# Attention on one core: the values' rounded and rest halves as one stationary tile, two products instead of three

## The chip, the cores and the metric

One core of a Trainium2 chip runs the whole program as one launch. The metric is the device time of that launch in microseconds (us), lower is better. Three runs of the kernel before took 1016.07, 1016.13 and 1017.07 us; their median is 1016.13.

The engines are called by the profile's names: PE is TensorE (its weight loads are listed apart as PEld), DVE is VectorE, ACT is ScalarE, POOL is GpSimd. Each runs its instructions in the order in which they were written into its queue and waits at semaphores for the others.

## The reference

A decoder trunk of two layers on 512 tokens of width 1024: a gated short convolution with a SwiGLU block, then an attention layer with a second SwiGLU block. Only the attention matters here. It has 16 heads of 64 columns; four heads share one of 4 key and value heads; a token sees the 128 tokens up to itself, and a sink joins the softmax.

```python
kk, vv = with_prev(k), with_prev(v)          # per block of 128: the block before and this one
scores = jnp.einsum('bnqhgd,bnkhd->bnhgqk', qb, kk).astype(jnp.float32) * scale
scores = jnp.where(valid[None, :, None, None], scores, NEG)
probs = jax.nn.softmax(jnp.concatenate([scores, sink], axis=-1), axis=-1)[..., :-1]
out = jnp.einsum('bnhgqk,bnkhd->bnqhgd', probs.astype(v.dtype), vv)
```

Everything is float32.

## The kernel before, in words

Each float32 operand of a product is cut into a rounded half, which ScalarE writes in the type fp32r, and a rest half, which VectorE makes by subtracting. A product of two operands is then three products (`mm3`, lines 193 to 195): rounded by rest, rounded by rounded, rest by rounded. Rest by rest is dropped.

The attention runs by pairs of heads. The heads are ordered so that pair t (of eight) holds two heads e = 0, 1 that use two neighbouring value heads. A loop of ten steps, i = 0 to 9, is written as one string, `ORDER`; each word of it is one piece of work of one pair, and the word order is the order in every engine's queue. In step i the words do the following:

- `R-` rotates the query projection of pair i + 1: on VectorE a shuffle (L1261) and a multiply (L1263), both reading the projection's PSUM tile, then two operations on POOL (L1267, L1270). `H-` splits the rotated queries (L1280 on ScalarE, L1281 on POOL).
- `S0`, `S1` are the scores of pair i, two halves of two PSUM tiles `psc`, one for each head (L1334). `M` masks and takes the maxima on VectorE (L1346), `E` the exponents on ScalarE (L1362, L1369), `N` divides by the sums on VectorE (L1374 to L1379).
- `T0` to `T3` transpose the probabilities of pair i - 1, one key block each (L1391), into the PSUM tiles `pt`; `P` writes their rounded half on ScalarE (L1404), `L` the rest half on VectorE (L1408).
- `W0` to `W3` (`weigh`) are the value products of pair i - 1, one key block each: per block and head three products of 128 x 256 into one PSUM tile `po`. The stationary tile is 128 wide though a head has 64 value columns: the value tiles `vt` hold zeros between the heads, so that head 0 fills the upper 64 partitions of `po` and head 1 the lower 64, each adding zeros to the other's. Thus 24 products a pair.
- `O-` (`out`) reads the finished `po` of pair i - 2 and writes its rounded half (ACT, L1428) and rest half (DVE, L1429), the operands of the output projection.
- `Q` projects the queries of pair i + 2 into a tile `pq`; `Z` and `z` (steps 5 to 8) compute the part of the output projection that needs only the first four pairs, and copy it out (L1446, `mixo`); `G`, `g`, `A` split weights ahead (L182 to L189, L420, L425).

For the steps in `NEXT` (0, 1, 2, 3, 4, 6, 7) `S1` is moved up behind `S0`, and its two tiles then come from the pool `ps_mm`; otherwise from `ps_sc`. `ps_mm` has four banks. It serves `S1` in those steps, `Q`, `Z` and `po`. A tile gets the bank that has been given back longest, and its first product waits until the last reader of the tile before it is done. `pt` has two banks of its own, `S0` two.

After the loop `close` finishes the output projection with pairs 4 to 7 (PSUM tiles `pmix`), pair 7 last.

## Time and profile before

| | us |
|---|---|
| median of three runs | 1016.13 (1016.07 to 1017.07) |
| profiled execution, span from its first to its last instruction | 1014.9 |
| between that span and the median: start and end around the instructions, since no separate device time is given for the profiled execution | 1.2 |
| PE busy in the span | 1007.0 (99%) |
| DVE, ACT, POOL busy | 867.8, 580.4, 193.8 |
| the loop's steps 1 to 8, first score product of step 1 to last value product | 555.31 to 653.67 |
| mean granted TensorE clock | 0.998 |

Times inside the execution count from the first instruction. In a row of the order of time the first number is the start, the second the duration, then engine, line, operation, output and inputs; `x4` merges four that follow each other, and square brackets give idle time ahead of it and what ended it. Matmuls overlap, so their pace is the distance between starts and not the duration. In a table by windows, each engine has its busy time and its number of instructions, and then come the granted clock, the share of DMA time and GB/s.

### The profile page before, as it was taken

To read this page: it belongs to the slowest core of one execution; us is meant where nothing else is said; L and a number is where in the kernel's file an instruction comes from. 1 tells how busy PE (TensorE), PEld (TensorE's weight loads), DVE (VectorE), ACT (ScalarE), POOL (GpSimd) and SP (SyncE) were. 2 spreads that over 40 slices of the span, in tenths; PEclk is the share of its full clock that TensorE was granted. 3 is DMA by queue.
4 is the path that set the end of the run, shared out by engine and by line. 5 is a ranking of instruction groups with operands and counts; after the bars stand their busy time and mean duration, and the time that the engine had idled before them with its cause. 6 is when DMAs were issued, how large, how long until landed. Compare 5 with 4: busy or idle time off the path is not lost.

```text
span 1014.9 us, 16253 instructions
## 1 busy us (share of the span) xinstructions
PE 1007.0 (99%) x6008; PEld 893.2 (88%) x6008; DVE 867.8 (86%) x1480; ACT 580.4 (57%) x1035; POOL 193.8 (19%) x259
## 2 busy tenths in 40 slices
PE   9999999999999999999999999999999999999997
PEld 8888888999889898998898888889998998989986
DVE  5766768899788999998878998779997899999896
ACT  6322544875656455566484786677666564645641
POOL 0443133102101011000032753221111010110001
PEclk9999999999999999999999999999999999999999
DMA  9897789549979789779603889976989676979842
GB/s 353 289 246 242 184 253 337 176 166 269 340 238 291 241 285 321 239 212 336 203 2 136 215 241 271 252 276 151 279 282 333 170 248 225 300 263 263 266 155 84
DMA packets 66576, 244.50 MB, mean 241 GB/s; under 512 B 7873, under 2 KB 8385, under 8 KB 54721
## 3 DMA queue, kind: packets, MB, share of 16 engines
q1 hardware_dynamic: 51328, 145.98, 38.8%
q0 software_dynamic: 14592, 96.48, 37.6%
q10 hardware_dynamic: 576, 1.02, 0.3%
q8 instruction: 47, 0.77, 0.3%
q14 instruction: 33, 0.26, 0.1%
HBM read 237.15 MB, written 102.76 MB: 335 GB/s over the span
## 4 chain that ended last, share of the span: by engine, by line
PE 99%; DVE 1%; issue 0%; DVEq 0%
PE gx L1072 15%; PE gx L1075 8%; PE gz L195 4%; PE gz L193 4%; PE gz L194 4%; PE pcub L193 4%; PE pcub L195 4%; PE pcub L194 4%; PE px L193 4%; PE px L194 4%; PE px L195 4%; PE pmix L193 3%; PE pmix L195 3%; PE pmix L194 3%; PE gy L195 2%; PE gy L194 2%
## 5 line engine op out<-in xcount | busy, mean ns | idle before, releaser
L479 DVE TENSOR_TENSOR wlo<-raw,whi 128x1024 fp32r<-128x1024 f32 x225 | 274.6, 1225 | 53.6 <-ACT whi L478 53.4
L478 ACT ACTIVATE whi<-raw 128x1024 fp32r<-128x1024 f32 x225 | 233.6, 1051 | 100.7 <-DVE raw L466 28.9
L1072 PE MATMUL gx<-xt,whi 128*128 128x512 f32 x480 | 120.4, 393 | 0.0
L1072 PEld LDWEIGHTS gx<-xt,whi 128*128 128x128 f32 x480 | 86.3, 189 | 15.5
L547 POOL DMA_DIRECT2D hsum<-in_w_gb_dram x96 | 62.8, 733 | 150.6 <-ACT whi L478 90.1
L547 POOL DMA_DIRECT2D hsum<-hsum x32 | 25.3, 790 | 295.5 <-ACT whi L478 198.2
L1034 DVE TENSOR_TENSOR st<-gx,st 128x256 f32<-128x256 f32 x200 | 78.0, 419 | 2.5 <-ACT st L1050 0.4
L1050 ACT ACTIVATE st<-gx 128x256 f32<-128x256 f32 x120 | 43.4, 380 | 62.6 <-PE gx L1075 58.9
L1075 PEld LDWEIGHTS gx<-xt,wlo 128*128 128x128 f32 x480 | 65.5, 190 | 4.7
L1075 PE MATMUL gx<-xt,wlo 128*128 128x256 f32 x480 | 66.9, 282 | 0.0
L1086 ACT ACTIVATE gr<-gr 128x1024 f32<-128x1024 f32 x20 | 21.2, 1062 | 49.9 <-DVE gr L1034 49.9
L193 PE MATMUL px<-wlo,ahi 128*128 128x512 f32 x120 | 46.7, 389 | 0.0
L194 PE MATMUL px<-whi,ahi 128*128 128x512 f32 x120 | 46.7, 389 | 0.0
L195 PE MATMUL px<-whi,alo 128*128 128x512 f32 x120 | 46.7, 389 | 0.0
L195 PE MATMUL gz<-xhi,wlo 128*128 128x256 f32 x160 | 45.5, 284 | 0.0
L193 PE MATMUL gy<-xlo,whi 128*128 128x256 f32 x160 | 45.3, 283 | 0.0
L194 PE MATMUL gy<-xhi,whi 128*128 128x256 f32 x160 | 45.3, 283 | 0.0
L195 PE MATMUL gy<-xhi,wlo 128*128 128x256 f32 x160 | 45.3, 283 | 0.0
L193 PE MATMUL gz<-xt,whi 128*128 128x256 f32 x160 | 45.3, 283 | 0.0
L194 PE MATMUL gz<-xt,whi 128*128 128x256 f32 x160 | 45.3, 283 | 0.0
L195 PE MATMUL gz<-xt,wlo 128*128 128x256 f32 x160 | 45.3, 283 | 0.0
L193 PE MATMUL gz<-xlo,whi 128*128 128x256 f32 x160 | 45.3, 283 | 0.0
(298 smaller groups left out, 2989.0 us busy)
## 6 DMA issues: line engine op xcount, KB each, us to landing
hsum<-in_w_gb_dram POOLq DMA_DIRECT2D x96, 512.0 KB, 7.8
raw<-hsum SPq DMA_DIRECT2D x88, 512.0 KB, 8.0
raw<-in_w_gb_dram SPq DMA_DIRECT2D x60, 512.0 KB, 7.0
hsum<-in_w_dn_dram POOLq DMA_DIRECT2D x36, 512.0 KB, 8.0
raw<-in_w_dn_dram SPq DMA_DIRECT2D x32, 512.0 KB, 6.3
hsum<-hsum POOLq DMA_DIRECT2D x28, 512.0 KB, 5.6
raw<-in_w_in_dram SPq DMA_DIRECT2D x21, 512.0 KB, 7.4
hsum<-in_w_dn_dram POOLq DMA_DIRECT2D x12, 768.0 KB, 12.9
```

What stands on the lines that cost most here:

```text
L193: nc.tensor.matmul(out, whi, xlo, start=start, stop=False, **kw)
L194: nc.tensor.matmul(out, whi, xhi, start=False, stop=False, **kw)
L195: nc.tensor.matmul(out, wlo, xhi, start=False, stop=stop, **kw)
L478: self.begun = nc.scalar.activation(hi[:, :n], raw, AF.Copy)
L479: nc.vector.tensor_tensor(out=lo[:, :n], in0=raw, in1=hi[:, :n].bitcast(F32), op=ALU.subtract)
L547: nc.gpsimd.dma_start(dst, src, max_dma_last_dim=4 * 4 * S, **kw))
L1034: nc.vector.tensor_tensor(out=out, in0=a, in1=b, op=ALU.add)
L1050: nc.scalar.activation(ste, a, AF.Copy)
L1072: nc.tensor.matmul(banks[c][e], whi[:, kk], factors[p][k][2], start=opened and k == 0, stop=False, **kw)
L1075: nc.tensor.matmul(banks[c][e][:, :256], wlo[:, kk], factors[p][k][0], start=False, stop=k == 3 and p == 4, **kw)
L1086: nc.scalar.activation(kept[2], kept[2], AF.Silu)
```

## The change

The value tiles change their layout. For each pair of value heads (g) a tile now holds four groups of 64 columns: rounded half of head 0, rest of head 0, rest of head 1, rounded of head 1. There are no zeros left, so the eight memsets of `vt` on POOL go, and four tiles of 128 x 512 hold what eight held. ScalarE writes groups 0 and 3 and VectorE groups 1 and 2 of each, in as many instructions as before.

One stationary tile of a head is now its rounded and its rest columns side by side. `weigh` multiplies it with the rounded probabilities and then with the rest ones: two products a head and block, 16 a pair, and rest by rest is now included. Each head has its own PSUM tile: for head 0 the upper 64 partitions hold the rounded values' part and the lower 64 the rest values' part, for head 1 the other way round.

A new piece, `join`, stands where `out` stood (`O-`): ScalarE copies the part of each tile that lies on the other half of the partitions across into an SBUF tile `o` (64 x 512, twice), and VectorE adds the part that lies where it belongs (64 x 512, twice). `out` (now `o-`) follows three words later, behind `M0` and `Q1`, and reads `o` in SBUF where it read `po` in PSUM.

```diff
-    "R- S0 T0 T1 O- Q0 M0 Q1 Z0 P0 P1 S1 ...
+    "R- S0 T0 T1 O- Q0 M0 Q1 o- Z0 P0 P1 S1 ...
...
         def weigh(self, j):
             if j == 0:
-                self.po = bank("po", ps_mm)
+                self.po = [bank("po", ps_mm) for _ in range(2)]
             hk = 2 * (self.t // 4)
-            phi, plo = self.turned[j][:2]
             q = min(j, NB - 2) * P
+            for i, p in enumerate(self.turned[j][:2]):
+                for e in range(2):
+                    nc.tensor.matmul(self.po[e][:, q : q + 256],
+                                     vt[j][:, (hk + e) * P : (hk + e + 1) * P],
+                                     p[:, e * 256 : (e + 1) * 256], start=i == j == 0,
+                                     stop=i == 1 and j == NB - 1, skip_group_check=True)
+
+        def join(self):
+            self.o = wide("o")[:, :S]
+            rows = [slice(e * HD, (e + 1) * HD) for e in range(2)]
             for e in range(2):
-                vc = slice((2 * hk + e) * HD, (2 * hk + 2 + e) * HD)
-                pc = slice(e * 256, (e + 1) * 256)
-                mm3(self.po[:, q : q + 256], vt[j][0][:, vc], vt[j][1][:, vc],
-                    phi[:, pc], plo[:, pc], j == 0 and e == 0, j == NB - 1 and e == 1,
-                    skip_group_check=True)
+                nc.scalar.activation(self.o[rows[e]], self.po[e][rows[1 - e]], AF.Copy)
+            for e in range(2):
+                nc.vector.tensor_tensor(out=self.o[rows[e]], in0=self.po[e][rows[e]],
+                                        in1=self.o[rows[e]], op=ALU.add)
...
-            nc.scalar.activation(hi, self.po, AF.Copy)
-            nc.vector.tensor_tensor(out=lo, in0=self.po, in1=hi.bitcast(F32), op=ALU.subtract)
+            nc.scalar.activation(hi, self.o, AF.Copy)
+            nc.vector.tensor_tensor(out=lo, in0=self.o, in1=hi.bitcast(F32), op=ALU.subtract)
...
-        vt = [halves("vt", F32R) for _ in range(NB)]
-        for pair in vt:
-            for v in pair:
-                nc.gpsimd.memset(v.bitcast(F32), 0.0)
+        vt = [v for _ in range(NB // 2) for v in halves("vt", F32R)]
...
-            nc.scalar.activation(dst[j][0], src[j], AF.Copy)
+            nc.scalar.activation(dst[j][:, :, 0::3], src[j], AF.Copy)
...
-            nc.vector.tensor_tensor(out=dst[j][1], in0=src[j], in1=dst[j][0].bitcast(F32),
-                                    op=ALU.subtract)
+            nc.vector.tensor_tensor(out=dst[j][:, :, 1:3], in0=src[j],
+                                    in1=dst[j][:, :, 0::3].bitcast(F32), op=ALU.subtract)
```

Two places show how the instructions move. A name's number tells tiles apart; `[waits ...]` names the engines on whose progress the instruction waits.

On TensorE, at the scores of step 2: where the second half's two tiles (from `ps_mm`) are opened and their next two products, before:

```order
L1334 MATMUL psc_5953<-rlo_5583,rhl_5869 128x256
L1334 MATMUL psc_5954<-rlo_5583,rhl_5869 128x256
L1334 MATMUL psc_5953<-rhi_5582,rhl_5869 128x256
L1334 MATMUL psc_5954<-rhi_5582,rhl_5869 128x256
L1334 MATMUL psc_5953<-rhi_5582,rhl_5869 128x256
```

and now:

```order
L1334 MATMUL psc_5936<-rlo_5573,rhl_5859 128x256
L1334 MATMUL psc_5937<-rlo_5573,rhl_5859 128x256 [waits DVE_49]
L1334 MATMUL psc_5936<-rhi_5572,rhl_5859 128x256
L1334 MATMUL psc_5937<-rhi_5572,rhl_5859 128x256
L1334 MATMUL psc_5936<-rhi_5572,rhl_5859 128x256
```

The second tile has gained a wait on VectorE. With `po` in two banks, the bank that it gets is that of the projection of step 1, which VectorE reads in this step's `R-`; in steps 3 and 4 it is the same.

On VectorE, the start of step 2, before (the second half of each row of maxima is a short instruction that reads an accumulator):

```order
L1261 STREAM_SHUFFLE sh_5932<-pq_5808 128x512 [waits PE_49]
L1263 TENSOR_TENSOR ra_5934<-pq_5808,ctab_5215 128x512 [waits PE_49]
L1429 TENSOR_TENSOR ohl_5981<-po_5891,ohl_5981 128x512 [waits Activation_49]
L1346 ISA s_5992,nm_5991<-psc_5939,mask,nsnk 128x128 [waits PE_49]
L1346 ISA nm_5991 128x1
```

and now, down to the rest half of the first transposed block:

```order
L1261 STREAM_SHUFFLE sh_5915<-pq_5798 128x512 [waits PE_49]
L1263 TENSOR_TENSOR ra_5917<-pq_5798,ctab_5215 128x512 [waits PE_49]
L1428 TENSOR_TENSOR o_5964<-po_5881,o_5964 64x512 [waits Activation_49]
L1428 TENSOR_TENSOR o_5964<-po_5882,o_5964 64x512 [waits Activation_49]
L1346 ISA s_5977,nm_5976<-psc_5922,mask,nsnk 128x128 [waits PE_49]
L1346 ISA nm_5976 128x1
L1346 ISA s_5978,nm_5976<-psc_5923,mask,nsnk 128x128 [waits PE_49]
L1346 ISA nm_5976 128x1
L1346 ISA s_5977,nm_5976<-psc_5922,mask,nsnk 128x256
L1346 ISA nm_5976 128x1
L1346 ISA s_5978,nm_5976<-psc_5923,mask,nsnk 128x256
L1346 ISA nm_5976 128x1
```

The two adds of the join stand where the rest half of the output stood, and that comes next after these rows, behind the maxima, as L1437. On ScalarE the two copies (L1426) stand where the rounded half (L1428) stood, and the rounded half follows them at once (L1436), ahead of the probabilities' rounded halves.

More of the change, by code (lines that the diff above doesn't have):

```diff
@@ L47 @@
 ORDER = (
-    "R- S0 T0 T1 O- Q0 M0 Q1 Z0 P0 P1 S1 T2 T3 L0 Q2 L1 G M1 E00 E01 k H- g0 Q3 P2 P3 E10 E11 Z1 z0 W0 L2 L3 A A A N0 W1 W2 N1 W3 g1 z1"
+    "R- S0 T0 T1 O- Q0 M0 Q1 o- Z0 P0 P1 S1 T2 T3 L0 Q2 L1 G M1 E00 E01 k H- g0 Q3 P2 P3 E10 E11 Z1 z0 W0 L2 L3 A A A N0 W1 W2 N1 W3 g1 z1"
 )
@@ L52 @@
     "S": "scores", "M": "maxima", "E": "exponents", "N": "normalise", "T": "turn", "P": "high",
-    "L": "low", "W": "weigh", "O": "out", "Q": "project", "R": "rotate", "H": "split",
+    "L": "low", "W": "weigh", "O": "join", "o": "out", "Q": "project", "R": "rotate", "H": "split",
     "G": "weights", "Z": "project", "z": "out",
@@ L1521, in yoco_kernel @@
         qs[0].rotate(nc.vector)
-        dst = [[v.rearrange("p (h d) -> p h d", d=2 * HD)[:, :, :HD] for v in pair]
-               for pair in vt]
-        src = [p.rearrange("p (h d) -> p h d", d=HD) for p in pv]
+        dst = [v.rearrange("p (g a d) -> p g a d", g=2, d=HD) for v in vt]
+        src = [p.rearrange("p (g e d) -> p g e d", g=2, d=HD) for p in pv]
         for j in range(NB):
-            nc.scalar.activation(dst[j][0], src[j], AF.Copy)
+            nc.scalar.activation(dst[j][:, :, 0::3], src[j], AF.Copy)
         for j in range(NB):
@@ L1563, in yoco_kernel @@
                     continue
-                if op in "SMENTPLWO":
-                    t -= op in "TPLWO"
+                if op in "SMENTPLWOo":
+                    t -= op in "TPLWOo"
                     of = hp
```

## The prediction

> **What bounds the kernel now.** I read the page's head and its chain that ended last, then the loop over the head pairs as a table by step, then the order of time inside one step.
>
> ```profile
> span 1014.9 us, 16253 instructions
> PE 1007.0 (99%) x6008; PEld 893.2 (88%) x6008; DVE 867.8 (86%) x1480; ACT 580.4 (57%) x1035; POOL 193.8 (19%) x259
> PE 99%; DVE 1%; issue 0%; DVEq 0%
> ```
>
> TensorE sets the end nearly everywhere, so fewer products should be time won. But these shares are means. The windows below run from a step's first score product to the next one's: rows 1 to 7 are steps 1 to 7 of the loop, the last row is step 8.
>
> ```profile
> core 0: us, PE busy (x) PEld busy (x) DVE busy (x) ACT busy (x) POOL busy (x), PEclk, DMA share, GB/s
> 555.31:567.00 11.69, 11.69 (x87) 10.34 (x86) 11.48 (x42) 8.05 (x28) 7.85 (x8) 1.00 0.85 244
> 567.00:578.69 11.69, 11.69 (x87) 10.36 (x86) 11.55 (x38) 8.38 (x27) 7.54 (x7) 1.00 0.88 247
> 578.69:590.39 11.70, 11.70 (x87) 10.36 (x86) 11.32 (x38) 8.88 (x28) 6.96 (x7) 1.00 0.92 197
> 590.39:602.17 11.78, 11.78 (x87) 10.41 (x86) 11.52 (x36) 10.01 (x29) 7.48 (x9) 1.00 0.64 164
> 602.17:619.61 17.44, 17.44 (x113) 14.85 (x112) 14.61 (x48) 9.91 (x31) 8.44 (x7) 1.00 1.03 345
> 619.61:631.49 11.88, 11.88 (x89) 10.41 (x88) 10.33 (x32) 10.17 (x32) 3.10 (x4) 1.00 0.88 209
> 631.49:643.38 11.89, 11.89 (x87) 10.36 (x87) 10.76 (x38) 10.21 (x32) 3.44 (x5) 1.00 1.01 290
> 643.38:653.67 10.29, 10.20 (x65) 8.83 (x63) 8.05 (x17) 7.52 (x12) 2.12 (x4) 1.00 0.96 276
> ```
>
> In steps 1 to 4 TensorE is busy throughout, and VectorE for all but 0.2 to 0.4 us of 11.7: two engines are full at once. Only steps 5 to 8 leave VectorE 1.1 to 2.8 us. So what the change adds to VectorE counts as much as what it takes from TensorE.
>
> **What it removes.** The value products, in order of time and by count:
>
> ```profile
> 565.84 0.28 PE L193 MATMUL po<-plo,vt 128*128 128x256 f32 x1
> 565.96 0.28 PE L194 MATMUL po<-phi,vt 128*128 128x256 f32 x1
> L193 PE MATMUL po<-plo,vt x48: 277/283/387, 564.0 to 652.6; 128*128 128x256 f32 x48
> L193 PE MATMUL po<-lp,vt x16: 280/283/283, 566.2 to 653.3; 128*128 128x256 f32 x16
> ```
>
> One lasts 0.28 us but the next starts 0.12 later, and that pace is the price. Lines 193 to 195 hold 64 each; the change leaves 128 of 192, so it takes 64 x 0.12 = 7.7 us, 0.96 a pair, in steps 1 to 8. The new products have the same shape and one weight load each; I keep the pace.
>
> Eight memsets on POOL go too. They are worth nothing: behind them POOL waits 24.7 us for VectorE's first rotation.
>
> ```profile
> 519.50 3.79 POOL L1503 MEMSET vt<- 128x512 f32 x8
> 548.97 1.29 POOL L1267 TENSOR_TENSOR sh<-sh,stab 128x512 f32<-128x512 f32 x1 [24.74 <-DVE sh L1261]
> ```
>
> The split of the values keeps its eight instructions and sizes: nothing.
>
> **What it adds to VectorE.** Step 2 shows the places, and the starts of the rotation in steps 3 to 5:
>
> ```profile
> 567.64 0.74 DVE L1261 STREAM_SHUFFLE sh<-pq 128x512 f32<-128x512 f32 x1
> 567.82 0.28 PE L1334 MATMUL psc<-rlo,rhl 64*128 64x256 f32 x2
> 568.27 0.68 DVE L1263 TENSOR_TENSOR ra<-pq,ctab 128x512 f32<-128x512 f32 x1
> 568.86 0.69 DVE L1429 TENSOR_TENSOR ohl<-po,ohl 128x512 fp32r<-128x512 f32 x1
> 569.46 0.35 DVE L1346 CUSTOM_DVE_ANT_0 s<-psc,mask,nsnk 128x128 f32<-128x128 f32 x1
> 570.81 1.29 DVE L1408 TENSOR_TENSOR plo<-pt,phi 128x512 fp32r<-128x512 f32 x2
> 579.31 0.75 DVE L1261 STREAM_SHUFFLE sh<-pq 128x512 f32<-128x512 f32 x1
> 591.02 0.74 DVE L1261 STREAM_SHUFFLE sh<-pq 128x512 f32<-128x512 f32 x1
> 604.67 0.75 DVE L1261 STREAM_SHUFFLE sh<-pq 128x512 f32<-128x512 f32 x1
> ```
>
> The low half of the output (L1429) takes 0.60 us, from 568.86 to the next start. It stays, only later. The two adds of the join have its 512 columns and one PSUM operand, on 64 partitions. No row shows 64 partitions on VectorE: below, 0.30 each if time went by elements; above, the whole 0.69. I take 0.60, since a row's columns pass one after another whatever the partitions. So 1.2 us a pair, first in step 2 (the join comes two steps behind its scores). VectorE's idle time there, 0.1 in step 2 and 0.3 to 0.4 in the next two, can't hold it, and I leave that idle time where it is, because it ends on other engines' work. So its chain grows by 1.2 in each of steps 2, 3 and 4, and the rotations of steps 3, 4 and 5 move from 579.31, 591.02 and 604.67 to 580.5, 593.4 and 608.3. With 0.30 an add they would move half as far, with 0.69 a sixth farther.
>
> **Who waits for that.** The pool of four banks gave a step four tiles (two score tiles, one projection, one output), so each kept its bank; now it gives five, and they wander. One of the score tiles opened at 567.82 falls on the bank of the projection that VectorE has yet to rotate; the product now carries a wait on VectorE that it did not have. In step 2 TensorE comes 0.96 early (one shorter weighing behind it) and stands until the multiply at 568.27 ends, 568.95: instead of 0.96 ahead it is 1.1 behind. In steps 3 and 4 the same product ran 0.2 after the shuffle's start (the step's window begins at 578.69 and 590.39, plus 0.82 as in step 2: 579.5 and 591.2). Now it starts with the end of the late multiply, 1.3 after the late shuffle: 581.8 and 594.7, so 2.3 and 3.5 behind. Queued behind it are the rest of the scores, the transposes and the next projection, and for these wait the maxima and the probabilities' halves. The shorter weighing at the end of step 4 gives back 0.96 unless it waits for the low half of its probabilities, which is as late as VectorE, 3.6: step 5 starts 2.6 to 3.6 late; I take 3.2, nearer the upper end, for ScalarE's queue has two copies more and feeds the same halves. With 0.30 an add the two stands leave 1.7 and 2.3 instead, and step 5 starts about 1.4 late.
>
> **Steps 5 to 8** win 4 x 0.96 = 3.8. Against it stands a longer path from the weighing to the next pair's probabilities: two copies on ScalarE, two adds, then the high half, before the probabilities' halves on both queues. A copy is taken at 0.5 to 0.6 (row 632.22 below; up to twice that for the unseen move across partitions). The places where nothing is spare:
>
> ```profile
> 629.66 0.28 PE L195 MATMUL po<-phi,vt 128*128 128x256 f32 x1
> 629.87 0.39 PE L193 MATMUL po<-plo,vt 128*128 128x256 f32 x1
> 632.22 0.59 ACT L1446 ACTIVATE mixo<-pe 128x512 f32<-128x512 f32 x1
> 632.30 0.28 PE L1334 MATMUL psc<-rlo,rhl 64*128 64x256 f32 x2
> 568.63 1.09 PE L1391 MATMUL pt<-ident,s 128*128 128x128 f32 x8
> 643.38 1.39 PE L1391 MATMUL pt<-ident,s 128*128 128x128 f32 x8
> ```
>
> Step 5: the early output product reads the newest pair's low half, which now comes behind the maxima; I put 0.3. Step 6: the third key block starts 0.21 after its neighbour, not 0.12, so it waits for VectorE already; the two shorter blocks before it bring TensorE there 0.48 sooner, and VectorE comes 0.6 later (1.2 of adds, half of it taken up by the 1.5 it has idle in that window): 1.1. Step 7: the second score tile takes the bank of the copy at 632.22, which ends 0.5 after the product wants it, and with ScalarE's longer queue 1.0. Step 8: its first eight transposes take 1.39 against 1.09 in step 2, so they wait for the normalising; with the next ones behind the probabilities' halves, 1.4. Together 3.8: the gain is used up. Bounds: 0 and 6.
>
> **The last pair** is covered.
>
> ```profile
> 653.87 0.60 ACT L1428 ACTIVATE ohi<-po 128x512 fp32r<-128x512 f32 x1 [0.26 <-PE po L195]
> 654.68 0.68 DVE L1429 TENSOR_TENSOR olo<-po,ohi 128x512 fp32r<-128x512 f32 x1
> 657.78 0.39 PE L193 MATMUL pmix<-wlo,ohi 128*128 128x512 f32 x1
> ```
>
> Its output is wanted at 657.78, 4.1 us after its last value product (653.67, where the windows end). Two copies 1.1, two adds 1.2 less 0.5 of overlap with the second copy, the halves 0.60 and 0.68: 3.1, and with 0.1 at each handing over some 3.5. That leaves 0.6; each delay beyond it would show in full.
>
> **Sum.** 3.2 - 3.8 + 3.8 = 3.2 us after the loop; the closing stages are TensorE's own and only shift. The profiled execution has a span of 1014.9; the median of the runs is 1016.13, 1.2 more lying around it. So span 1018.1, time 1019.3 us.
>
> **Shared port.** The moved low half reads the joined tile from SBUF, no longer PSUM.
>
> ```profile
> 575.36 1.29 POOL L1270 TENSOR_TENSOR ra<-ra,sh 128x512 f32<-128x512 f32 x1
> 575.69 0.98 DVE L1374 TENSOR_TENSOR se<-se,rs 128x4 f32<-128x4 f32 x1
> 569.83 1.30 POOL L1270 TENSOR_TENSOR ra<-ra,sh 128x512 f32<-128x512 f32 x1
> ```
>
> A 4-column add with both operands in SBUF lasts 0.98 and ends with POOL's add (575.36 + 1.29 = 576.65). The low half will start 3.8 after the shuffle (1.2 rotation, 1.2 adds, 1.35 maxima); POOL's rotation ends at 571.13, 3.5 after it. Spare: 0.3. If POOL is later, VectorE loses up to 1.0 in each of steps 2 to 6. The Trainium skill, "SBUF — State Buffer", section "Who interferes with whom", says that a VectorE instruction with two SBUF inputs contends with a GpSimd one reading SBUF, one with at most one such input does not. By that rule, the trace agrees: L1429 with its PSUM operand ran its 0.69 at 568.86 beside POOL.
>
> **Rivals.** (1) Hidden after step 5, 0.15: the waits of steps 5 to 8 vanish in ScalarE's and VectorE's spare time there; 3.2 - 3.8 = -0.6, 1015.5 us (1014.5 to 1017.5). For: 1.1 to 2.8 us spare in the windows. Against: the waits are of order, not load. (2) Faster, 0.06: the adds cost no more than VectorE's idle 0.2 to 0.4 a step, that is, under 0.2 each. Then steps 1 to 4 win what VectorE leaves (0.2 + 0.1 + 0.4 + 0.3 = 1.0) and steps 5 to 8 win 3.8: 1011.3 us. For: TensorE has no slack at all, so all of it would show. Against: 512 columns from PSUM cost 0.60. (3) Slower still by the shared port, 0.12: two more us, 1021.5. (4) Clock, 0.04.
>
> ```profile
> 1005.00:1014.90 9.90, 3.13 (x26) 2.89 (x24) 6.01 (x12) 1.24 (x4) 1.27 (x2) 0.76 0.27 107
> ```
>
> With TensorE busy 3.1 of the last 9.9 us, the granted clock falls to 0.76. Stalls of about 2 us in steps 2 to 4 could do it: at 0.76 a step with 10.7 us of products loses 2.6, two such steps 5, so 1024.5 us. Against it: TensorE stays over 80% busy in a step of 12.9. The Trainium skill, "TensorE: Matmul & The Clock Gate", Part 1, puts the fall after an idle window of about 3.4 us; by it these stalls are too short. That the products are not saved at all is excluded: their number falls in the order of the program.
>
> **Chances.** The forecast has 0.63, range 1017.5 to 1021.5. About 0.2% (2 us) is what a measurement of this kernel tells from no change: 1014.1 to 1018.2. Forecast: 0.54 slower, 0.09 same. Rival 1: 0.12 same, 0.02 faster, 0.01 slower. Rival 2 faster, 3 and 4 slower. So faster 0.08, same 0.21, slower 0.71. The range of 8 in 10 takes in rival 1's upper part and rival 3: 1015.8 to 1022.0.
>
> **What would show it.** In the changed profile: value products 128 at 0.12; TensorE's first waits of the loop at the second score tile of steps 2 to 4, released by VectorE's L1263 line, each 1 to 2.3 us; VectorE 99% busy in steps 2 to 4 with steps of 12.9 us; adds at 0.60 to 0.69; a granted clock of 1.00 in the loop. Adds near 0.3, or steps of 11 us, would make the prediction wrong.

## The result, and the profile after

The changed kernel takes 1024.14 us (median of four runs, 1023.20 to 1024.80) against 1016.26 us for the kernel before on the same chip: a ratio of 1.0075, 95% interval 1.0062 to 1.0088. The prediction said 1019.3 us with a range of 1015.8 to 1022.0. The direction is right, the size is not: +7.9 us instead of +3.2, above the range. The two profiled executions, whose rows follow, are 7.0 us apart by their spans; the other 0.9 lies between them and the medians.

The page's head and its chain that ended last, after:

```profile
span 1021.9 us, 16136 instructions
PE 1005.3 (98%) x5944; PEld 888.4 (87%) x5944; DVE 879.1 (86%) x1496; ACT 589.6 (58%) x1051; POOL 190.2 (19%) x251
PE 91%; DVE 7%; ACT 2%; issue 0%; DVEq 0%; ACTq 0%
```

64 products are gone (6008 to 5944), but TensorE's busy time falls by only 1.7 us, and 9% of the chain is now VectorE and ScalarE, where it was 1%.

The loop by step, cut as in the prediction, from a step's first score product to the next one's (the last row ends before the first closing product, at 660.16):

```profile
core 0: us, PE busy (x) PEld busy (x) DVE busy (x) ACT busy (x) POOL busy (x), PEclk, DMA share, GB/s
554.75:565.49 10.74, 10.74 (x80) 9.39 (x79) 10.60 (x38) 8.06 (x29) 7.81 (x8) 1.00 0.82 232
565.49:580.00 14.51, 12.66 (x81) 10.95 (x80) 13.52 (x42) 9.70 (x30) 7.49 (x8) 0.88 0.84 221
580.00:592.44 12.44, 11.10 (x79) 9.55 (x78) 12.06 (x36) 9.89 (x30) 6.76 (x8) 1.00 0.85 166
592.44:607.13 14.69, 12.67 (x79) 10.89 (x78) 13.61 (x41) 10.99 (x32) 7.70 (x10) 0.88 0.76 202
607.13:624.34 17.21, 16.78 (x105) 13.90 (x104) 16.42 (x52) 11.34 (x34) 6.33 (x6) 1.00 1.02 323
624.34:635.77 11.43, 10.99 (x80) 9.45 (x80) 10.68 (x31) 10.54 (x33) 5.58 (x7) 1.00 0.85 169
635.77:649.09 13.32, 11.87 (x79) 9.59 (x79) 12.34 (x41) 11.78 (x36) 2.61 (x4) 1.00 1.03 275
649.09:659.50 10.41, 9.23 (x49) 7.16 (x50) 8.39 (x19) 7.33 (x13) 3.40 (x6) 1.00 0.87 257
```

Step 1 wins the 0.95 us that its products are worth (11.69 to 10.74). Steps 2 to 4 last 41.64 us together instead of 35.17: 6.47 lost. Steps 5 to 8, from 607.13 to 660.16, last 53.03 instead of 51.50: 1.53 lost although they too have 3.8 us of products less. Together that is +7.05; the loop started 0.56 us earlier than before (554.75 for 555.31), which is the spread between executions and no gain of the change: the kernels below that are equal ahead of the loop start it some 0.7 us apart. So the first closing product comes 6.5 us later, and the span ends 7.0 later. In rows 2 and 4 the granted clock is 0.88: TensorE ran part of these steps at half clock.

What TensorE waited for in the loop (total, number of times, longest):

```profile
PE psc L1334 <- DVE ra L1263: 5.2, 3, 2.0
PE pt L1391 <- DVE plo L1408: 1.3, 2, 0.9
PE psc L1334 <- ACT mixo L1454: 1.0, 1, 1.0
PE po L1417 <- DVE plo L1408: 0.4, 1, 0.4
PE pe L195 <- DVE ohl L1437: 0.4, 1, 0.4
PE pt L1391 <- DVE s L1379: 0.2, 1, 0.2
```

Before, the same view had no row of TensorE. The first is the wait that the prediction named: the second score tile on the bank of the projection that VectorE has yet to rotate. Step 2 in order of time:

```profile
566.30 0.28 PE L1334 MATMUL psc<-rlo,rhl 64*128 64x256 f32 x1
567.08 0.72 DVE L1261 STREAM_SHUFFLE sh<-pq 128x512 f32<-128x512 f32 x1
568.29 1.40 DVE L1428 TENSOR_TENSOR o<-po,o 64x512 f32<-64x512 f32 x2
568.43 0.38 PE L1334 MATMUL psc<-rlo,rhl 64*128 64x256 f32 x1 [1.84 <-DVE ra L1263]
569.59 1.97 PE L1391 MATMUL pt<-ident,s 128*128 128x128 f32 x8
581.08 0.72 DVE L1261 STREAM_SHUFFLE sh<-pq 128x512 f32<-128x512 f32 x1
```

TensorE stands 1.84 us; then its eight transposes take 1.97 us where they took 1.09 before. The next rotation starts 14.0 us after this one. Before, it was 11.67 (567.64 to 579.31).

### The profile page after: what moved, and what is told of

It is laid out like the page before. It is cut to its first block, busy times and chain, and to the rows that moved or that the text cites. A ratio compares the mean times of both kernels' runs of the same rounds, so it can differ in the third digit from the quotient of the medians.

```text
span 1021.9 us, 16136 instructions
## 1 busy us (share of the span) xinstructions
PE 1005.3 (98%) x5944; PEld 888.4 (87%) x5944; DVE 879.1 (86%) x1496; ACT 589.6 (58%) x1051; POOL 190.2 (19%) x251
## 4 chain that ended last, share of the span: by engine, by line
PE 91%; DVE 7%; ACT 2%; issue 0%; DVEq 0%; ACTq 0%
PE gx L1072 14%; PE gx L1075 7%; PE gz L195 4%; PE gz L193 4%; PE gz L194 4%; PE pcub L194 4%; PE pcub L193 4%; PE pcub L195 4%; PE px L194 4%; PE px L193 4%; PE px L195 4%; PE pmix L195 3%; PE pmix L193 3%; PE pmix L194 3%; PE gy L194 2%; PE gy L193 2%
```

## Experiments

Two questions were open after this. Is it VectorE's load (the two adds) or the bank that lengthens steps 2 to 4? And what does the half clock cost? All kernels are compared with the kernel before on the same chip. "Steps 2 to 4" is the time from the first score product of step 2 to that of step 5, "steps 5 to 8" from there to the first closing product, both read from the order of time of each profile.

| kernel | us | ratio to before, 95% interval | steps 2 to 4 | steps 5 to 8 |
|---|---|---|---|---|
| before | 1016.3 | 1 | 35.17 | 51.50 |
| the change | 1024.14 | 1.0075 (1.0062 to 1.0088) | 41.64 | 53.03 |
| e1 small adds | 1019.17 | 1.0030 (1.0018 to 1.0041) | 41.93 | 50.43 |
| e2 before, two banks | 1021.07 | 1.0045 (1.0030 to 1.0060) | 38.85 | 52.39 |
| e3 before, two adds | 1020.22 | 1.0038 (1.0023 to 1.0053) | 37.22 | 53.34 |
| e4 stall filled | 1023.16 | 1.0064 (1.0049 to 1.0079) | 39.75 | 53.31 |
| e7 scores later | 1022.27 | 1.0057 (1.0040 to 1.0074) | 39.20 | 53.31 |
| e8 scores later, small adds | 1015.79 | 0.9994 (0.9984 to 1.0003) | 36.11 | 50.46 |
| e6 pairs 4 to 7 alone | 1018.15 | 1.0019 (1.0010 to 1.0029) | 35.17 | 52.30 |
| e9 e7, low half on POOL | 1024.06 | 1.0073 (1.0058 to 1.0088) | 39.69 | 53.35 |
| e10 more on POOL | 1027.58 | 1.0109 (1.0092 to 1.0126) | 42.92 | 53.50 |
| e11 e7, out later | 1019.06 | 1.0031 (1.0020 to 1.0043) | 37.04 | 52.13 |
| e12 e11, weights on POOL | 1025.45 | 1.0089 (1.0074 to 1.0104) | 43.31 | 53.27 |
| e13 pairs 4 to 7, ordered | 1016.10 | 0.9991 (0.9982 to 1.0001) | 35.20 | 50.45 |

### The adds made small

```diff
-                nc.vector.tensor_tensor(out=self.o[rows[e]], in0=self.po[e][rows[e]],
-                                        in1=self.o[rows[e]], op=ALU.add)
+                nc.vector.tensor_tensor(out=self.o[rows[e], :16], in0=self.po[e][rows[e], :16],
+                                        in1=self.o[rows[e], :16], op=ALU.add)
```

> The changed kernel, but the join's two adds on VectorE cover 16 of 512 columns; the other 496 columns of the output lack the part that should be added. Banks, products and order stay. Load theory (the adds' 1.4 us a step make VectorE late, and TensorE with it): the stall of TensorE at the second score tile of step 2 stays at 1.8 us, because it lies ahead of the first add, and with it one stretch at half clock (1.6 us); in steps 3 and 4 the stalls fall to under 1.2 us and there is no second stretch; 1017.7 to 1020. Bank theory (the fifth tile puts TensorE behind the rotation however long the adds are): stalls of 1.8, 1.3 and 2.0 us as now, two stretches at half clock; 1022.5 to 1024.

1019.17 us. The time lies in the range of the load theory, but the place is wrong. The three stalls of the second score tile, in order of time:

```profile
568.54 0.58 PE L1334 MATMUL psc<-rlo,rhl 64*128 64x256 f32 x1 [1.82 <-DVE ra L1263]
582.89 0.38 PE L1334 MATMUL psc<-rlo,rhl 64*128 64x256 f32 x1 [1.76 <-DVE ra L1263]
595.79 0.58 PE L1334 MATMUL psc<-rlo,rhl 64*128 64x256 f32 x1 [1.78 <-DVE ra L1263]
```

With 1.0 us less of adds a pair, steps 2 to 4 are as long as with them (41.93 to 41.64). What was won lies in steps 5 to 8 (50.43 to 53.03). So in steps 2 to 4 of this execution the adds are not what sets the time, and after step 5 they are. The profiled execution is the slowest of seven, at 1021.0 us with two stretches at half clock; the others, with mean clocks of 0.996 to 0.999, took 1018.95 to 1020.28. So part of the 5.0 us between the medians may be half clock that most executions of this kernel were spared; no profile shows one of them.

### One part alone: the bank, and the adds

The kernel before with a second output bank a pair:

```diff
-                self.po = bank("po", ps_mm)
+                self.po, self.po2 = [bank("po", ps_mm) for _ in range(2)]
...
+                if e == j == 0:
+                    nc.tensor.matmul(self.po2[:, :256], vt[j][0][:, vc], phi[:, pc],
+                                     start=True, stop=True)
...
+            nc.vector.tensor_copy(out=lo[:, :16], in_=self.po2[:, :16])
```

> The kernel before with one part of the change alone: each pair also takes a second bank for its output (one extra value product of 128x256 writes it, and a VectorE copy of 16 columns reads it where the low half of the output is made). The second score tile of steps 2 to 4 then falls on the bank of the projection, as in the changed kernel. Load theory: TensorE is not ahead here, so one stall of about 1.1 us in step 2, none over 0.5 us in steps 3 and 4, clock 1.00 in the loop; with 8 extra products (1.0 us) and the later waits on the copies of the early output 1018 to 1019.5. Bank theory: stalls of over 1.3 us in each of steps 2 to 4, half clock at least once; 1021 or more.

The kernel before with two adds a pair:

```diff
+            for r in (slice(0, HD), slice(HD, P)):
+                nc.vector.tensor_tensor(out=lo[r], in0=self.po[r], in1=hi[r].bitcast(F32),
+                                        op=ALU.add)
             nc.vector.tensor_tensor(out=lo, in0=self.po, in1=hi.bitcast(F32), op=ALU.subtract)
```

> The kernel before with VectorE's load alone: two more adds of 64x512 a pair (PSUM operand, written to the tile of the low half, which is then written over), just before the low half of the output. Banks and products as before. Load theory: VectorE's step grows by 1.4 us from step 2 on, steps 2 to 4 last about 13.0 us instead of 11.7, TensorE waits for the normalised probabilities and the halves; with part of it taken up from step 5 on 1019.5 to 1021.5, stalls each under 1.4 us and no half clock. Bank theory: without the bank VectorE's delay is mostly hidden; 1016.5 to 1018.

Each part alone costs about half of what both cost: 1021.07 us with the bank, of which some 1.0 are its eight products more (8 x 0.12), and 1020.22 with the adds. The adds first: the time lies in the range of the load theory (1019.5 to 1021.5) and far above the bank theory's 1016.5 to 1018, but steps 2 to 4 last 12.53, 12.29 and 12.40 us and not the 13.0 of that theory. So the load is real, and smaller than I put it.

With the bank alone, my load theory wanted one stall of 1.1 us and then none, and the bank theory stalls of over 1.3 us and the half clock. The time is in the bank theory's range, just; the stalls fit neither, and the clock stays at 1.00 in the loop. The stalls are small, 0.75, 0.75 and 0.77 us, but they come back in every step, and the steps last 12.93, 12.95 and 12.97 us without either engine being full. Steps 2 to 4 as windows:

```profile
566.49:579.42 12.93, 12.18 (x88) 10.65 (x87) 12.06 (x40) 8.37 (x27) 7.50 (x7) 1.00 0.83 218
579.42:592.37 12.95, 12.20 (x89) 10.66 (x88) 11.64 (x40) 8.87 (x28) 6.94 (x7) 1.00 0.76 173
592.37:605.34 12.97, 12.20 (x90) 10.65 (x89) 11.79 (x37) 10.05 (x29) 7.47 (x9) 1.00 0.74 198
```

VectorE (third pair of numbers) is idle for 0.9 to 1.3 us of each, TensorE (first pair) for 0.8. Step 3 of the kernel with two banks, in order of time:

```profile
579.91 0.73 DVE L1261 STREAM_SHUFFLE sh<-pq 128x512 f32<-128x512 f32 x1
581.26 0.38 PE L1334 MATMUL psc<-rlo,rhl 64*128 64x256 f32 x1 [0.75 <-DVE ra L1263]
582.17 1.09 PE L1391 MATMUL pt<-ident,s 128*128 128x128 f32 x8
582.92 1.09 ACT L1404 ACTIVATE phi<-pt 128x512 fp32r<-128x512 f32 x2 [2.80 <-PE pt L1391]
588.01 0.58 ACT L1404 ACTIVATE phi<-pt 128x512 fp32r<-128x512 f32 x1
588.62 0.69 DVE L1408 TENSOR_TENSOR plo<-pt,phi 128x512 fp32r<-128x512 f32 x1 [0.79 <-ACT phi L1404]
592.88 0.73 DVE L1261 STREAM_SHUFFLE sh<-pq 128x512 f32<-128x512 f32 x1
```

This is a **circle**. The scores wait for the rotation; behind them in TensorE's queue stand the transposes; for these ScalarE waits 2.80 us with the probabilities' high halves; at the end of its queue for the step comes the third block's high half, for which VectorE waits 0.79 us with the low half; behind that VectorE normalises, and behind that stands the next rotation. From the rotation to the transposes it takes 2.26 us (579.91 to 582.17), from there to the next rotation 10.71: 12.97, the length of the step. In the kernel before the second part was as long (568.63 to 579.31, 10.68), but the transposes came 0.99 behind the rotation and waited for nothing of it. The sum 2.26 + 10.7 could have been read from the rows of before: it is 1.3 us more than a step of 11.7, in each of three steps, and the value products, which the change makes fewer, are not on it.

### The half clock

```diff
+                if half and n == 2 and self.t in (2, 3, 4):
+                    for _ in range(12):
+                        nc.tensor.matmul(pss[0][:, cc], qhi[rows[0], q], klo[rows[0], kk],
+                                         start=True, stop=True)
```

> The changed kernel with 12 more score products in each of steps 2, 3 and 4, put on TensorE just before the product that waits for the rotation: copies of the next product, written over by it, 0.12 us each, so 1.4 us of work that nobody needs in the place of idle time. Clock theory (the half clock comes from the length of the idle time): no stall in these steps over 0.7 us, granted clock 1.00 in the whole loop, 1019.5 to 1022 although TensorE has 36 products more. Rival (the clock falls for another reason, the load of the stretch behind it): the half clock stays, and the time is that of the changed kernel or up to 1 us more: 1023.5 to 1025.

```profile
569.15 0.38 PE L1338 MATMUL psc<-rlo,rhl 64*128 64x256 f32 x1 [0.42 <-DVE ra L1263]
582.29 0.38 PE L1338 MATMUL psc<-rlo,rhl 64*128 64x256 f32 x1 [0.60 <-DVE ra L1263]
595.43 0.38 PE L1338 MATMUL psc<-rlo,rhl 64*128 64x256 f32 x1 [0.59 <-DVE ra L1263]
```

The idle time falls to 0.42 to 0.60 us, and the clock stays at 1.00 through the whole loop: the half clock does come from the idle time. But the kernel gains 1.0 us only (1024.14 to 1023.16), which lies between the ranges of the two theories. 1.9 us come out of steps 2 to 4, and 1.6 out of the whole loop, from its first rotation to the first closing product; the steps still last 13.0, 13.2 and 13.6 us. Two stretches of 3.4 us at half clock hold 3.4 us of work back, so about half of that lay under waits that were there anyway.

### The circle opened, with and without the adds

```diff
-                order = order.replace("S1 ", "").replace("S0 ", "S0 S1 ")
+                after = "Q1 " if i in (1, 2, 3, 4) else "S0 "
+                order = order.replace("S1 ", "").replace(after, after + "S1 ")
```

> The changed kernel with one word moved: in steps 1 to 4 the second half's scores stand behind the first two quarters of the projection (Q1) instead of behind the first half's scores, so that TensorE comes to them about 3.7 us later, when the rotation that holds their bank is long done. Loop theory (rotation, second scores, transposes, probabilities, normalising, next rotation are tied into a circle by the bank, 12.9 us a step whatever the adds cost): no stall over 1 us at the second scores of steps 2 to 4, no half clock; what is left is VectorE's load of 12.9 us a step (11.5 and 1.4 of adds) and the waits of steps 5 to 8, 1018 to 1021. Load theory (VectorE's adds alone set steps 2 to 4): the same lateness through the normalised probabilities, 1021 to 1023.5, less only the half clock's share of 3 us.

> The same move, and the join's two adds on 16 of 512 columns, so that the other 496 columns of the output lack the part that should be added: neither the circle nor the load. Loop theory: steps 2 to 4 at 11.0 to 11.7 us (VectorE 11.5 and 0.3), 1010.5 to 1013.5. If the small adds gain nothing against the same kernel with whole adds, the load does not count even without the circle.

1022.27 and 1015.79 us. The wait for the rotation is gone from both, but with whole adds the idle time has only moved: TensorE now waits 4.1 us in five places for the low halves, the longest in step 3:

```profile
586.01 1.03 PE L1391 MATMUL pt<-ident,s 128*128 128x128 f32 x6 [1.78 <-DVE plo L1408]
```

Behind it the clock is at 0.50 from 587.25 to 590.66, where the loop theory had said that no half clock would be left. With whole adds the kernel is only 1.9 us faster than the change, in the range of the load theory and 1.3 us above that of the loop theory; with small ones it falls by 6.5 us, but stops 2.3 us above its range. Without the first circle the adds do count: 3.1 us in steps 2 to 4 (39.20 to 36.11) for three times 1.03 us less of adds. From one rotation to the next it is 13.13 and 13.11 us with whole adds and 12.09 and 12.11 with small ones, 1.0 less a round, and the half clock in step 3 made no round longer. Load, or again order? That decides what would help, so the next kernels take work off VectorE.

### Work moved from VectorE to POOL

```diff
-            nc.vector.tensor_tensor(out=lo, in0=self.o, in1=hi.bitcast(F32), op=ALU.subtract)
+            eng = nc.gpsimd if self.t < KT - 1 else nc.vector
+            eng.tensor_tensor(out=lo, in0=self.o, in1=hi.bitcast(F32), op=ALU.subtract)
```

> The kernel with the later scores of the second half (e7_scores_later), and the low half of the output for the pairs 0 to 6 on POOL instead of VectorE, which the join makes possible since its operand lies in SBUF; POOL takes about 1.3 us where VectorE took 0.60. Load theory without the circle (1.1 us less of adds a pair gave 6.5 us): 0.6 us less a pair gives about 3.5, 1018 to 1019.5. Rival (POOL's operation delays VectorE's on SBUF operands, or comes late behind the rotation): 1020.5 to 1022.5.

The next one adds:

```diff
-NEXT = (0, 1, 2, 3, 4, 6, 7)
+NEXT = (0, 1, 2, 3, 4, 6)
...
-            self.w = split_weights(w_q[self.t])
+            self.w = split_weights(w_q[self.t], eng=nc.gpsimd if self.t > 3 else None)
```

> As e9_low_on_pool, and two more: the rest halves of the query weights of pairs 4 to 7 (128x1024, 1.22 us on VectorE in steps 1 to 4) on POOL, and in step 7 the second half's scores at their late place with the banks of the first half, so that they don't wait for the early output's copy (1.0 us). Load theory: VectorE's step in steps 1 to 4 falls from 12.9 to 11.1 us, below the 11.7 of the kernel before; steps 2 to 4 under 11.7 us, step 7 about 1 us less: 1012.5 to 1016, faster than the kernel before if at the lower end. Rival (POOL with 11.4 us in 11 becomes the next engine that sets the steps, through the split of the rotated queries): 1017 to 1021.

Both are slower than without, and above the ranges of both theories: 1024.06 and 1027.58 us. In these two kernels it is not VectorE's load that sets steps 2 and 3. Step 3 of the second as a window:

```profile
579.77:593.04 13.27, 11.88 (x79) 9.40 (x78) 11.07 (x39) 9.61 (x31) 11.26 (x11) 1.00 0.78 157
```

VectorE has 11.07 us of work in 13.27, and still its rotations stand 13.1 us apart, as in the first. Step 3 of the first, in order of time:

```profile
580.76 0.73 DVE L1261 STREAM_SHUFFLE sh<-pq 128x512 f32<-128x512 f32 x1
583.41 0.63 ACT L1436 ACTIVATE ohl<-o 128x512 fp32r<-128x512 f32 x1 [3.62 <-DVE o L1428]
583.95 1.06 ACT L1404 ACTIVATE phi<-pt 128x512 fp32r<-128x512 f32 x2
589.64 0.69 DVE L1408 TENSOR_TENSOR plo<-pt,phi 128x512 fp32r<-128x512 f32 x1 [0.67 <-ACT phi L1404]
593.90 0.73 DVE L1261 STREAM_SHUFFLE sh<-pq 128x512 f32<-128x512 f32 x1
```

ScalarE stands 3.62 us for the join's adds, with the output's high half at the head of its queue. The probabilities' high halves, whose transposes have long been there, stand behind it. This is a **second circle**: rotation and adds on VectorE (2.65 us), the output's high half on ScalarE (0.54), from the probabilities' high halves to the third block's low half (5.69), from there to the next rotation (4.26): 13.14. The adds are in it, VectorE's low half is not. It runs through the place of the new `o-` in ScalarE's queue. That the second of these kernels is 3.5 us slower than the first lies for the most part ahead of the rotation of step 2, which comes 12.68 us behind that of step 1 in place of 10.31. There an add of four columns on VectorE lasts 3.31 us, and ends with POOL's third operation in a row (566.72):

```profile
563.44 3.31 DVE L1374 TENSOR_TENSOR se<-se,rs 128x4 f32<-128x4 f32 x1
```

Step 4 adds 0.8 us more. In step 7 the second score tile now waits 1.10 us for VectorE's maxima in place of 1.0 for the copy; nothing was won there.

### The second circle opened

```diff
+            if i != 5 and i <= KT:
+                order = order.replace("o- ", "").replace("L1 ", "L1 o- ")
```

> The kernel with the later scores (e7_scores_later), and the halving of the output, whose high half stands on ScalarE ahead of the probabilities' high halves and waits there for VectorE's adds, moved behind the low halves of the first two key blocks (all steps but 5 and the last). Theory of the second circle (rotation, adds, output's high half, probabilities' high halves on ScalarE, their low halves, normalising, next rotation: 13.1 us a step in the two kernels with work moved to POOL, however idle VectorE was): without it VectorE's load of 12.7 to 12.9 us a step is the next limit in steps 2 to 4, so 0.2 to 0.4 us a step less there, and steps 6 to 8 lose the waits of the transposes for the halves (0.4 and 0.85 us): 1019 to 1021. Rival (no second circle, the place doesn't matter): 1021.5 to 1023, as the kernel with the later scores alone.

> As e11_out_later, and the rest halves of the query weights of pairs 4 to 7 on POOL (1.22 us a step off VectorE in steps 1 to 4, 2.6 us more on POOL). Theory of the second circle: now that the circle is gone the load counts, VectorE's step is 11.6 us, steps 2 to 4 last 11.0 to 11.9 us: 1014 to 1017. Rival (taking work off VectorE gains nothing, as it gained nothing in the kernels before, 1024.1 and 1027.6): 1020 or more.

The move alone takes 3.2 us off (1022.27 to 1019.06), in the range of its theory. It moves VectorE's low half as well as ScalarE's high half, but the low half had been off VectorE in the two kernels above without any gain. Now VectorE's load is the limit; step 3 of that kernel as a window:

```profile
577.57:589.87 12.30, 11.28 (x79) 9.35 (x78) 12.10 (x40) 9.99 (x30) 7.39 (x8) 1.00 0.88 174
```

VectorE is busy for 12.10 of 12.30 us. Then taking 1.22 us off it should have paid, but the kernel that does so takes 1025.45, in the range of its rival. Its low half of the output, in steps 3 and 4, and what POOL did meanwhile:

```profile
586.38 2.38 POOL L189 TENSOR_TENSOR wlo<-raw,whi 128x1024 fp32r<-128x1024 f32 x1
587.28 2.03 DVE L1437 TENSOR_TENSOR ohl<-o,ohl 128x512 fp32r<-128x512 f32 x1
599.61 3.01 POOL L189 TENSOR_TENSOR wlo<-raw,whi 128x1024 fp32r<-128x1024 f32 x1
599.78 4.63 DVE L1437 TENSOR_TENSOR ohl<-o,ohl 128x512 fp32r<-128x512 f32 x1
601.98 1.88 POOL L1281 TENSOR_TENSOR rhl<-ra,rhl 128x512 fp32r<-128x512 f32 x1
```

The low half, 0.69 us long elsewhere, lasts 2.03 us beside one operation of POOL and 4.63 beside two, and ends both times 0.55 us behind POOL's last one (whose spans are rough). The add of four columns again lasts 3.31 us in step 1, and two windows behind 607.21 are at half clock. So that kernel says nothing on the load. What a lighter VectorE would give without POOL, with both circles open, was not tried.

All this can be read from one distance, that from the start of one rotation's shuffle (L1261) to the next, in us:

| kernel | steps 2 to 3 | 3 to 4 | 4 to 5 |
|---|---|---|---|
| before | 11.67 | 11.71 | 13.65 |
| e3, adds alone | 12.28 | 12.27 | 14.54 |
| e11, both circles open | 12.30 | 12.30 | 14.57 |
| e2, bank alone | 12.93 | 12.97 | 14.91 |
| e4, stall filled | 13.15 | 13.14 | 15.08 |
| e7, first circle open | 13.13 | 13.11 | 15.09 |
| e9, and low half on POOL | 13.14 | 13.14 | 15.54 |
| e10, and weights on POOL | 13.13 | 13.11 | 16.36 |
| the change | 14.00 | 13.13 | 15.85 |
| e1, the change, small adds | 14.35 | 12.90 | 16.33 |
| e8, first circle open, small adds | 12.09 | 12.11 | 14.05 |

There are three lengths: some 12.3 us where VectorE is full, 12.95 for the circle through the bank, 13.14 for the circle through ScalarE's queue. The longest that a kernel has sets its step. The change has all three, so the last sets it, and opening the first circle alone leaves the distance as it was (13.13); the half clock comes on top in steps 2 and 4. Step 3 of the change shows the second circle itself; the round begins with the shuffle at 581.08 above:

```profile
583.72 0.63 ACT L1436 ACTIVATE ohl<-o 128x512 fp32r<-128x512 f32 x1 [2.52 <-DVE o L1428]
589.95 0.69 DVE L1408 TENSOR_TENSOR plo<-pt,phi 128x512 fp32r<-128x512 f32 x1 [0.23 <-ACT phi L1404]
594.21 0.72 DVE L1261 STREAM_SHUFFLE sh<-pq 128x512 f32<-128x512 f32 x1
```

The parts are 2.64, 6.23 and 4.26 us, those of the kernel with the low half on POOL to 0.01. With small adds the second circle is 1.03 us shorter, 12.11: that is the distance in e8, and why it stopped above its range. In e1 the first circle is then the longest, 12.90 in the step without half clock.

### The change where VectorE has room

Pairs 4 to 7 alone, whose values are weighed in steps 5 to 8; then the same with the orders that the runs above suggest, and with the split of the values in four ScalarE instructions instead of eight:

```diff
+            if self.t < 4:
+                if j == 0:
+                    self.po = bank("po", ps_mm)
...
+                    mm3(self.po[:, q : q + 256], vz[j][0][:, vc], vz[j][1][:, vc],
```

> The change for the pairs 4 to 7 alone, whose values are weighed in steps 5 to 8, where VectorE has idle time; pairs 0 to 3 keep the three products, one bank and no join, with value tiles of their own (192 columns with zeros between the heads, eight small memsets on POOL and eight more small instructions in the split of the values). Steps 1 to 4 as before. Theory (steps 5 to 8 were slowed by the lateness that they inherited and by their own waits): the products of four pairs are 3.8 us less, the waits on the early output's copies in step 7 (1.0 us) and on the halves stay in part: 1013 to 1016. If the later waits of 3.8 us that the prediction put there are real by themselves: 1016 to 1017.

```diff
-                order = order.replace("S1 ", "").replace("S0 ", "S0 S1 ")
+                after = "P1 " if i > 5 else "S0 "
+                order = order.replace("S1 ", "").replace(after, after + "S1 ")
+            if i != 5 and i <= KT:
+                order = order.replace("o- ", "").replace("L1 ", "L1 o- ")
```

> The change for the pairs 4 to 7 alone (as e6_second_half), with what the runs showed put right: in steps 6 to 8 the halving of the output stands behind the first two low halves; in steps 6 and 7 the second half's scores stand behind the probabilities' high halves, so that their banks are free; and ScalarE writes the rounded halves of the values for both layouts in four instructions instead of eight. Theory: TensorE loses no more than 1.5 us of waits in steps 5 to 8 against products of 3.8 us less, and the loop starts 0.5 to 1 us later than in the kernel before for four more small VectorE instructions: 1014.5 to 1016.0, a little faster than the kernel before or equal to it. Rival (steps 5 to 8 of TensorE are set by VectorE's 46.5 us of work there and gain nothing): 1016.5 to 1018.

The first takes 1018.15 us, slower than both its cases: the loop starts 1.4 us later, and steps 5 to 8 last 52.30 us where they lasted 51.50, with 3.8 us of products less. So the waits of these steps cost 4.6 us by themselves, without any lateness from the steps before (in the profiled execution, which at 1019.63 us is 1.5 above the median). Put in order, they last 50.45 us, with one large wait left, of 1.1 us, the transposes' for a low half.

That kernel takes 1016.10 us, 0.1 above its range and below its rival's, a ratio of 0.9991 (0.9982 to 1.0001): no difference that can be told from the kernel before. No version was found that beats it.

## Why the prediction was right or wrong

**Products, memsets, copies: right.** The value products of a pair take 2.00 us after (16, from 563.49 to 565.49), so 0.9 less than before, and step 1 shows all of it. The copies from the other half of the partitions last 0.59 us, within the 0.5 to 0.6 taken.

**The adds: mis-sized by a fifth.** I took 0.60 us each from the pace of the low half; one lasts 0.69, and the two take 1.43 (568.29 to 569.72). 64 partitions save nothing over 128.

**The second score tile behind the rotation: right in place, releaser and size.** Stalls of 1 to 2.3 us in steps 2 to 4 were said; 1.84, 1.34 and 2.02 were seen.

**"The rotations of steps 3, 4 and 5 move" by the adds' 1.2 us each: this is the step that failed.** It let VectorE's chain grow by its own work alone and made TensorE its follower. The adds alone lengthen the round by 0.6 us and not 1.2: VectorE fills up at 12.3, because its 11.5 us before held time lost to POOL. The add of four columns that the prediction shows, 0.98 us long beside POOL's add in step 2, takes 0.14 there once the two adds have moved it. What lengthens the change's round to 13.14 us is order: the wait of ScalarE's high half for the adds, and next to it the wait at the bank, which with no adds at all gives 12.95. Both come back to VectorE's next rotation. I had the halves of the first circle in the rows quoted and never asked whether the waiting product lies ahead of what releases it in the next step. So the 12.9 us a step that I forecast is near the 13.1 by chance.

**Where the missing time is.** The rotations of steps 2 and 5 were to stand 40.6 us apart (37.03 and 3.6), and stood 42.98. With the stall filled it is 41.37, so 1.6 us of this miss is the half clock, which the forecast put at nothing, and 0.7 the longer round. As the loop also began 0.56 us earlier, step 5 starts 5.0 us late (607.13 for 602.17) and not 3.2. Steps 5 to 8 lose 1.5 where gain and waits were to be even, the end 0.5, and 0.9 lies outside the profiled spans: together the 4.7 us between +3.2 and +7.9.

**The output's move behind the maxima: costed on VectorE, not on ScalarE.** The prediction counts two copies more in ScalarE's queue, but gives no price to the high half that waits there for the adds, ahead of the probabilities' high halves: the second circle. Once the first was open, that place cost 3.2 us.

**Steps 5 to 8: right in kind, too small.** I set 3.8 us of waits against 3.8 won. The waits seen are 0.43 in step 5 (0.3 said), 0.44 in step 6 (1.1), 1.01 in step 7 for the early output's copy (1.0), and 1.1 in step 8 (1.4), but also 0.39 in step 7 for the low halves, and after each stop the first products run without overlap. Alone they cost 4.6 us, in the change 5.4; the waits listed are 3.4 of that, and the rest is not traced to single rows.

**The last pair: not quite covered.** I gave it 0.6 us to spare. The first closing product comes 6.5 us later than before and the end of the span 7.0, so up to 0.5 us shows; a weight load of the closing products waits 0.4 us for the last low half.

**The shared port: not at the low half.** It ran its 0.69 us in every step. The mechanism is real, though, as the 2.03 and 4.63 us above show; the spare 0.3 was enough.

**The clock: given 0.04, and it happened**, in two steps of the profiled execution. My reason against it was that TensorE stays over 80% busy in such a step; the row shows that the step is the wrong interval to ask. Its price was misjudged too: I put 5 us on two such steps, and taking both away gave 1.6 in the loop and 1.0 in the time. The 0.76 in the row quoted was a mean: the clock was 1.00 up to 1010.18 and 0.50 behind it, as in the loop here. That the rival's 1024.5 us is near the result is chance: it was added to a forecast that lacked both circles, at three times its price.

## What to carry to other kernels

When a change makes a tile share a bank with one that another engine still reads, follow the new wait forward until it reaches its own releaser again; if it does, add up the way round, because a step can't be shorter than that sum, whatever work is saved beside it. Do so for every such circle: opening one gains nothing while another is as long. An instruction that waits for another engine, put at the head of an in-order queue, holds up all that stands behind it, and closes such a circle too. When one engine's spare time is 0.2 us a step, work taken from its neighbour and given to it is not a gain, and work pushed on to a third engine did not pay here, where the two met in memory (0.69 us became 4.63).

## What the runs showed of the hardware

**About half a window of idle time can be enough for the half clock.** In the changed kernel, by windows:

```profile
566.58:568.43 1.85, 0.01 (x2) 0.01 (x2) 1.85 (x7) 0.11 (x1) 0.55 (x1) 1.00 0.90 221
568.96:572.37 3.41, 3.41 (x18) 2.99 (x15) 3.35 (x13) 2.00 (x4) 2.23 (x3) 0.50 1.10 370
596.26:599.68 3.42, 3.42 (x17) 2.90 (x14) 3.39 (x12) 2.27 (x4) 3.34 (x5) 0.50 0.26 24
```

Each stretch lasts 3.41 to 3.42 us at exactly 0.50, and starts 0.5 to 0.7 us after TensorE is back at work. The two start 27.30 us apart, eight times 3.41; in the kernel with small adds they start at 568.44 and 595.74, again 27.30 apart. So the clock seems to be decided on a fixed grid of 3.41 us. On that grid the stalls of 1.84 and 2.02 us lie whole in the window ahead of a stretch and fill 54% and 59% of it; the one of 1.34 us fills 39% and has no stretch behind it. With small adds the stalls of 1.82 and 1.78 us lie with 1.72 and 1.73 in one window, 50% and 51%, and have one; that of 1.76 us, which the grid cuts into 0.96 and 0.80, has none. Three other kernels have such a stretch in the loop, behind windows that are 52%, 71% and 61% idle (e7, e10, e12), and of the windows in all the loops that have none behind them the most idle is the 39% above. But near the end of e13 the window from 1005.99 to 1009.40 is 54% idle, and the clock falls only after the next one, which is idle throughout. So the share of a window is not the whole rule; no kernel was made to test it. The Trainium skill, "TensorE: Matmul & The Clock Gate", Part 1, has a free-running window of 3413 ns and two states, half and full; the trace agrees. It has the clock fall after an idle window; here windows of which 41 to 50% were still busy were enough, and the measurement decides.

**POOL and VectorE on SBUF.** VectorE's low half with both operands in SBUF went from 0.69 to 2.03 and 4.63 us beside POOL's operations, and an add of four columns from 0.44 us in the kernel before to 3.31. The Trainium skill, "SBUF — State Buffer", section "Who interferes with whom", says that such a pair contends, and the trace agrees.
